# Three units share the first x tiles, and the unit of 36 features becomes 16 fp32 products on column halves

## The chip, the core and the metric

One Trainium2 chip, one of its cores. The metric is the device time of one launch in microseconds (us). The kernel's engines: TensorE does the matrix products (PE in the profile, its weight loads PEld), VectorE is DVE, ScalarE is ACT, GpSimd is POOL, and SyncE (SP) issues nearly all transfers from device memory.

## The reference

The kernel computes one layer of a hybrid encoder trunk on x of 256 tokens by 2048 features, in float32. Cut to what the change touches:

```python
u = _rms_norm(x, norm_mix_pre)                     # x * rsqrt(mean(x^2) + eps) * gain
proj = u @ w_in
sb, fox, rw, gates = _split(proj, ...)
q_a, k_a, v_a = _split(sb, (512,) * 3)             # stick-breaking attention, 4 heads of 128
q_b, k_b, v_b, f_b = _split(fox, ...)              # f_b: 4 forget logits per token
log_f = log_sigmoid(f_b + b_forget)
# RWKV-7: the projected features are mixed with those of the token before
z = z + (z_prev - z) * mu
r, k, v, wd, ad, gd = _split(z, (1024, 1024, 1024, 64, 64, 160))
g = sigmoid(gd) @ g_up
```

After that come the three mixers, three gated branches, an output projection with a second norm, and an MLP of 8192 hidden features. All of that is the same in both kernels.

## The kernel before

**A unit.** Nearly every projection is made in units of 128 output features. The weights of a unit are two pieces of the stream `wst`, each of 128 x 1024 floats (512 KB), and each piece covers eight of the 16 tiles of 128 input features. Products are not made in fp32: each operand is split into a rounded part ("hi", type fp32r) and the rest ("lo"). ACT writes the hi part of a weight piece (L173), DVE subtracts to get the lo part (L175). An input tile is split in the same way into a tile of 512 columns: the hi part of 256 tokens, then the lo part. A unit then needs, on PE, 16 products of hi weights with 512 columns (L191, the last one L197) and 16 of lo weights with 256 columns (L195). `evac` adds the two halves of the result (L249 on ACT, L250 on DVE).

**Streams and buffers.** SP issues the pieces in order into three `raw` tiles; a new piece waits until the lo part of the one three back is made. `whi` and `wlo` have three tiles each, and one piece is split ahead (`wnext`). Each `wnext` call that loads a piece also runs one function from the list `side`: constants, then the normalised x tiles.

**The begin.** x comes in transposed, as 16 tiles in eight transfers of 256 KB. The first two units (the first two heads of the stick-breaking q) are made from x tiles as they land: `xsplit` (L340, that is L259 on ACT and L260 on DVE) multiplies with the norm's gain and splits; the norm's factor per token, `rstd`, is not known yet and is multiplied into the results later (`scaled`, L465). The orders of PE, ACT and DVE are written out by hand in this part (L317 to L407): for each pair of x tiles, `high` (L345) and `low` (L349) of unit 0 and of unit 1. The pieces of these units come as column halves (pieces 0 and 2) and whole (pieces 1 and 3; piece 3 lies in a tile of the pool tag `m`). After the begin only PE keeps its written order; a scheduler orders ACT and DVE.

**Behind the begin.** Units 2 to 7 follow on the same x tiles. Between them lie the eight squares of x (L431 on ACT, seven adds L433 on DVE, in the tile `A6` of tag `b6`), the sum over features on PE behind unit 4 (L438), `rstd` (L440 to L275), and a small product that turns `rstd` into columns behind unit 6 (L457). Then comes v (`tok`, eight pieces, L235 and L220), and behind v the unit `zz`: 32 features of the gate LoRA and the four forget logits, 36 of its 128 columns, the others zero. It reads the normalised tiles `upk` and is made like any other unit; `shift` (L640) then mixes it with the token before. The units of the next projections follow. Mixer work is woven between the units by a count of ticks, four in a unit.

Of the kernel before, what the change touches and what calls it, by code (L numbers as in the profile page):

```python
# [11 lines left out]
F32 = mybir.dt.float32  # L12
F32R = mybir.dt.float32r
AF = mybir.ActivationFunctionType
ALU = mybir.AluOpType
# [3 lines left out]
T = 256  # L19
D = 2048  # L20
KT = 16
AHEAD = 1
SHARE = 0.88
HALF = 1024
# [7 lines left out]
PC = {}  # L32
# [20 lines left out]
def hybrid_block(ctx, tc, xt, x, gains, params, consts, lora, gup, wst, out):  # L53
    nc = tc.nc
    V, A, G, PE = nc.vector, nc.scalar, nc.gpsimd, nc.tensor

    cpool = ctx.enter_context(tc.tile_pool(name="cpool", bufs=1))
    wpool = ctx.enter_context(tc.tile_pool(name="wpool", bufs=1))
# [17 lines left out]
    def pk():  # L76
        return pkpool.tile([128, 512], F32R, tag="pk", name=nm("pk"), bufs=24)
# [6 lines left out]
    par = cpool.tile([128, NPAR], F32, name="par")  # L84
# [52 lines left out]
    def tick(f=1.0):  # L137
# [7 lines left out]
        if hooks:  # L145
# [3 lines left out]
    wpos = [0]  # L149


    gc = wst.shape[0] - 256 - 32 - 48
    jump = {23: 28, 53: 24, 27: 54, gc + 7: gc + 12, gc + 19: gc + 24, gc + 31: gc + 8,
            gc + 11: gc + 20, gc + 23: gc + 32}
    wq = []
    side = []

    rawdma = [None]

    def wraw(n=None):  # L160
# [9 lines left out]
    def wsplit(raw, n=None, now=True):  # L170
        hl = home[0](n) if home[0] else None
        hi, lo = hl or (wpool.tile([128, HALF], F32R, tag=t, name=nm(t), bufs=3) for t in ("whi", "wlo"))
        A.activation(hi, raw, AF.Copy)  # L173
        wq.append((hi, lo))
        low = lambda: V.tensor_tensor(lo, raw, hi.bitcast(F32), ALU.subtract)  # L175
        return low() if now else low
# [101 lines left out]
    rp = p1.enter_context(tc.tile_pool(name="rp", bufs=1))  # L278
# [7 lines left out]
    z = tmp()  # L286
    G.memset(z, 0.0)
    X0 = rp.tile([128, KT, T], F32, tag="SC", name="x0", bufs=1)
    A6 = rp.tile([128, 6, T], F32, tag="b6", name="a6", bufs=1)
    nc.scalar.dma_start(out=par, in_=params)  # L290

    dum = cpool.tile([128, 1], F32, name="dum")
# [3 lines left out]
    def xload(a, b):  # L296
        nc.sync.dma_start(out=X0[:, a:b, :], in_=xt[:, a:b, :])


    raws = {n: wpool.tile([128, HALF], F32, tag="raw", name=nm("raw"), bufs=3) for n in (0, 2)}  # L300
    for c in (0, 512):
        for n in (0, 2):
            nc.sync.dma_start(out=raws[n][:, c:c + 512], in_=wst[n][:, c:c + 512])
            xload(c // 128 + n, c // 128 + n + 2)
    raws[1] = wraw(1)
    xload(8, 10)
    xload(10, 12)

    raws[3] = rp.tile([128, 2, 512], F32, tag="m", name="raw3", bufs=4).rearrange("p a b -> p (a b)")
    nc.sync.dma_start(out=raws[3], in_=wst[3])  # L310
    xload(12, 14)
    xload(14, 16)
    cst = cpool.tile([128, 4], F32, name="cst")
# [11 lines left out]
    ps = mps()  # L325
# [16 lines left out]

    def high(u, *ks):
        for k in ks:
            PE.matmul(qb[u], w[u, k // 8][0][:, k % 8 * 128:k % 8 * 128 + 128], xpk[k], start=k == 0, stop=False)  # L345

    def low(u, *ks):
        for k in ks:
            PE.matmul(qb[u][:, 0:T], w[u, k // 8][1][:, k % 8 * 128:k % 8 * 128 + 128], xpk[k][:, 0:T], start=False,  # L349
                      stop=k == 15)  # L350

    qb = [gps() for _ in range(2)]
    w = {(u, 0): [wpool.tile([128, HALF], F32R, tag=t, name=nm(t), bufs=3) for t in ("whi", "wlo")] for u in range(2)}

    def part(u, c, lo):
        c = slice(c, c + 512)
        hi, raw = w[u, 0][0][:, c], raws[2 * u][:, c]
        if lo:
            V.tensor_tensor(w[u, 0][1][:, c], raw, hi.bitcast(F32), ALU.subtract)
        else:  # L360
            A.activation(hi, raw, AF.Copy)

    def both(u, *ks):
        high(u, *ks)
        low(u, *ks)

    for c in (0, 512):
        k = c // 128
        part(0, c, False)
        xsplit(k)  # L370
        xsplit(k + 1)
        part(1, c, False)
        high(0, k, k + 1)
        high(1, k, k + 1)
        part(0, c, True)
        if c == 0:
            part(1, c, True)
        low(0, k, k + 1)
        xsplit(k + 2)
        xsplit(k + 3)  # L380
        if c:
            part(1, c, True)
        low(1, k, k + 1)
        both(0, k + 2, k + 3)
        both(1, k + 2, k + 3)

    def whole(n):
        later = wsplit(raws.pop(n), None, False)
        return wq.pop(), later

    w[0, 1], later = whole(1)
    xsplit(8)
    xsplit(9)
    later()
    both(0, 8, 9)
    xsplit(10)
    xsplit(11)
    both(0, 10, 11)
    w[1, 1], later = whole(3)
    later()  # L400
    both(1, 8, 9, 10, 11)
    for k in (12, 14):
        xsplit(k)
        xsplit(k + 1)
        both(0, k, k + 1)
        both(1, k, k + 1)
    order.__exit__(None, None, None)  # L407
    order = tc.manual_schedule(engines={mybir.EngineType.PE})
    order.__enter__()
# [14 lines left out]
    wpos[0] = 4  # L424
    rstd = rp.tile([128, T], F32, tag="cs", name="rstd1", bufs=1)

    def square(i):
        xf = X0[:, 2 * i:2 * i + 2, :]
        b = 2 + 2 * (i % 2) if i else 0
        with tc.issue_after(behind[0].ins):  # L430
            A.activation(A6[:, b:b + 2, :], xf, AF.Square)  # L431
        if i:
            V.tensor_tensor(A6[:, 0:2, :], A6[:, 0:2, :], A6[:, b:b + 2, :], ALU.add)  # L433

# [10 lines left out]
    upk = [pk() for _ in range(KT)]  # L445
# [21 lines left out]
    todo = [lambda i=i: square(i) for i in range(8)] + [norm] + [lambda k=k: normed(k) for k in range(3)] + [column] +\  # L467
           [lambda k=k: normed(k) for k in range(3, 9)]
    for h, n in enumerate((0, 0, 4, 4, 1, 3, 4, 3)):
        ps = qb[h] if h < 2 else unit(xpk)  # L470
        qk.append(g1())
        behind[1] = evac(ps, qk[h])
        if h > 4:
            scaled(h)
        for f in todo[:n]:
            f()
        del todo[:n]

    def later(i):
        normed(9 + i)  # L480
        if i < 5:
            scaled(i)

    side.extend(lambda i=i: later(i) for i in range(7))
    done["sbq"], done["sbk"] = qk[:4], qk[4:]


# [70 lines left out]
    def fox_mix():  # L558
# [78 lines left out]
            yield ("stage", 0.8)  # L637
        done["yb"] = out

    def shift(ps, i, dst, n=128):  # L640

        b, t = tmp(), tmp()
        zp = rp.tile([128, T + 1], F32, tag="zp", name=nm("zp"), bufs=2)
        G.memset(zp[:, 0:1], 0.0)
        A.activation(b[0:n], ps[0:n, T:2 * T], AF.Copy)
        V.tensor_tensor(t[0:n], ps[0:n, 0:T], b[0:n], ALU.add)
# [331 lines left out]
    for br in ("sb", "fox"):  # L978
        for s in ("q", "k"):
            if br == "sb":  # L980
                continue
            lst = []
            for h in range(4):
                ps = unit(upk)
                t = g1()
                evac(ps, t)
                lst.append(t)
            done[br + s] = lst
        done[br + "v"] = vtok(br == "sb")
        done[br] = True  # L990
        for i, nme, n in ((0, "zx", 128), (1, "zy", 128)) if br == "fox" else ((2, "zz", 36),):
            ps = unit(upk)
            z = rp.tile([128, T], F32, tag="tha", name=nme, bufs=1) if i == 0 else \
                rp.tile([64 if n == 36 else n, T], F32, name=nme)
            shift(ps, MU_X + i, z[0:n], n)
            done[nme] = z
# [36 lines left out]
    for g in range(4):  # L1033
        m = rp.tile([128, 2, 512], F32, tag="m", name=nm("m"), bufs=4)
# [170 lines left out]
    low = more(False)  # L1205
# [454 lines left out]
```

## Time and profile before

| what | value |
|---|---|
| median of 3 runs | 1508.16 us (1507.34 to 1508.66) |
| the profiled execution, its own time | 1509.36 us |
| its span, first to last instruction | 1507.6 us |
| lies outside the span | 1.8 us |
| DVE busy | 1206.6 us (80%) |
| ACT busy | 939.8 us (62%) |
| DMA, mean over the span | 207 GB/s |

A busy engine is one with an instruction in work. A row of the timeline gives the start and the duration of a group of like instructions that follow each other, and how many there are; the last one's duration reaches into the next group's start, because products are pipelined. An fp32 product appears as two records of the PE, an fp32r product as one. The distance from one start to the next is therefore the cost of a product, not its duration.

### The profile page before, as it was taken

What the parts mean: (1) busy time and instruction counts of PE and PEld (TensorE: products, weight loads), DVE (VectorE), ACT (ScalarE), POOL (GpSimd) and SP (SyncE); (2) the same over time, 40 slices, a digit from 0 to 9 for tenths busy, and PEclk for the clock granted to TensorE, in tenths of its full rate; (3) what the DMA queues carried; (4) which work ended last, traced back from release to release, by engine and by line L of the source; (5) the groups of instructions that cost most, each with busy time, mean ns of one, the idle gap of its engine ahead of it and who ended that gap; (6) DMA issues with size and microseconds to landing.
All of it is one profiled execution on the core that took longest, in us unless ns stands there. A gap on an engine that the chain in (4) does not pass through costs nothing.

```text
span 1507.6 us, 22703 instructions
## 1 busy us (share of the span) xinstructions
PE 1492.0 (99%) x8384; PEld 1254.0 (83%) x8384; DVE 1206.6 (80%) x1673; ACT 939.8 (62%) x1433; POOL 94.5 (6%) x151
## 2 busy tenths in 40 slices
PE   9999999999999999999999999999999999999997
PEld 7888888887788887788888988888888888888886
DVE  7875679895678796476557778998899989999996
ACT  7665677545676445564545766776667666767663
POOL 0021003000001000000000000000000000000000
PEclk9999999999999999999999999999999999999999
DMA  7655454454455465456675768888888888989874
GB/s 263 197 168 184 142 182 154 154 182 163 156 165 177 154 192 186 130 169 196 231 238 159 265 177 254 229 242 273 263 259 258 244 254 248 258 254 258 246 224 152
DMA packets 104687, 312.71 MB, mean 207 GB/s; under 512 B 10240, under 2 KB 12288, under 8 KB 104576
## 3 DMA queue, kind: packets, MB, share of 16 engines
q1 hardware_dynamic: 93968, 279.87, 56.2%
q0 software_dynamic: 8064, 29.36, 10.5%
q10 hardware_dynamic: 2544, 2.03, 0.5%
q8 instruction: 66, 1.08, 0.3%
q14 instruction: 45, 0.37, 0.1%
HBM read 279.77 MB, written 2.10 MB: 187 GB/s over the span
## 4 chain that ended last, share of the span: by engine, by line
PE 89%; DMA 4%; DVE 2%; issue 2%; ACT 2%; POOLq 0%; SPq 0%; DVEq 0%; POOL 0%; ACTq 0%
PE gps L235 27%; PE gps L191 21%; PE gps L195 12%; PE gps L220 7%; PE mps L1378 3%; PE mps L1380 3%; PE mps L1379 3%; DMA raw<-in_wst_dram 2%; PE gps L1380 2%; PE gps L1378 2%; PE gps L1379 2%; DMA raw<-raw 2%; PE gps L197 1%; DVE wlo L175 1%; ACT whi L173 1%
## 5 line engine op out<-in xcount | busy, mean ns | idle before, releaser
L175 DVE TENSOR_TENSOR wlo<-raw,whi 128x1024 fp32r<-128x1024 f32 x576 | 699.0, 1224 | 159.2 <-ACT whi L173 147.3
L173 ACT ACTIVATE whi<-raw 128x1024 fp32r<-128x1024 f32 x576 | 604.1, 1057 | 260.4 <-PE gps L235 76.3
L191 PE MATMUL gps<-pk,whi 128*128 128x512 f32 x1479 | 375.6, 392 | 1.8 <-DVE tmp L1296 1.0
L191 PEld LDWEIGHTS gps<-pk,whi 128*128 128x128 f32 x1479 | 274.2, 188 | 57.9 <-ACT whi L173 2.3
L235 PE MATMUL gps<-whi,pk 128*128 128x512 f32 x1004 | 253.6, 393 | 0.0
L195 PEld LDWEIGHTS gps<-pk,wlo 128*128 128x128 f32 x1582 | 215.6, 190 | 15.6 <-DVE wlo L175 0.7
L195 PE MATMUL gps<-pk,wlo 128*128 128x256 f32 x1582 | 221.1, 283 | 0.1
L235 PEld LDWEIGHTS gps<-whi,pk 128*128 128x128 f32 x1004 | 186.6, 188 | 39.8 <-issue 1.0
L235 PE MATMUL gps<-wlo,pk 128*128 128x512 f32 x502 | 138.2, 393 | 0.1
L235 PEld LDWEIGHTS gps<-wlo,pk 128*128 128x128 f32 x502 | 93.2, 188 | 20.0 <-DVE wlo L175 0.5
L1378 PE MATMUL mps<-whi,fm 128*128 128x512 f32 x224 | 88.8, 396 | 0.8 <-ACT whi L173 0.6
L1295 ACT ACTIVATE tmp<-gps 128x256 f32<-128x256 f32 x64 | 24.6, 384 | 101.4 <-PE gps L197 99.5
L1379 PE MATMUL mps<-whi,fm 128*128 128x512 f32 x224 | 87.8, 392 | 0.0
L1380 PE MATMUL mps<-wlo,fm 128*128 128x512 f32 x224 | 87.6, 391 | 0.0
L1358 POOL DMA_DIRECT2D raw<-raw x56 | 48.8, 872 | 573.1 <-DVE raw L1355 279.5
L1355 DVE TENSOR_TENSOR raw<-raw,raw 128x1024 f32<-128x1024 f32 x56 | 68.5, 1222 | 0.8
L1378 PE MATMUL gps<-whi,fm 128*128 128x512 f32 x168 | 65.9, 392 | 0.0
L1380 PE MATMUL gps<-wlo,fm 128*128 128x512 f32 x168 | 65.9, 392 | 0.0
L1379 PE MATMUL gps<-whi,fm 128*128 128x512 f32 x168 | 65.5, 390 | 0.0
L220 PE MATMUL gps<-whi,pk 128*128 128x512 f32 x224 | 60.8, 393 | 0.0
L1380 PEld LDWEIGHTS mps<-wlo,fm 128*128 128x128 f32 x224 | 42.1, 188 | 9.7 <-DVE wlo L175 0.2
L1378 PEld LDWEIGHTS mps<-whi,fm 128*128 128x128 f32 x224 | 42.4, 189 | 8.9 <-ACT whi L173 2.9
(346 smaller groups left out, 1726.6 us busy)
## 6 DMA issues: line engine op xcount, KB each, us to landing
raw<-in_wst_dram SPq DMA_DIRECT2D x516, 512.0 KB, 4.4
raw<-raw POOLq DMA_DIRECT2D x56, 512.0 KB, 6.8
x<-in_xt_dram SPq DMA_DIRECT2D x8, 256.0 KB, 6.7
x<-in_x_dram SPq DMA_DIRECT2D x8, 256.0 KB, 4.7
raw<-in_wst_dram SPq DMA_DIRECT2D x4, 256.0 KB, 4.9
g<-in_gains_dram SPq DMA_DIRECT2D x4, 256.0 KB, 4.8
pk<-in_gains_dram SPq DMA_DIRECT2D x4, 256.0 KB, 6.9
out_dram<-x SPq DMA_DIRECT2D x4, 256.0 KB, 2.8
```

The source lines that it names most:

```text
L173: A.activation(hi, raw, AF.Copy)
L175: low = lambda: V.tensor_tensor(lo, raw, hi.bitcast(F32), ALU.subtract)
L191: PE.matmul(ps, hi[:, i * 128:i * 128 + 128], pks[i], start=first and i == 0, stop=False)
L195: PE.matmul(ps[:, 0:T], lo[:, i * 128:i * 128 + 128], pks[i][:, 0:T], start=False, stop=False)
L220: PE.matmul(ps[tt], pks[k][:, c:c + 128], w[:, (k - k0) * 512:(k - k0) * 512 + 512], start=k == 0 and part == 0 and w is hl[0], stop=w is ...
L235: PE.matmul(ps[tt], pks[k][:, c:c + 128], w[:, (k - k0) * 512:(k - k0) * 512 + 512], start=k == 0 and part == 0 and w is hl[0], stop=False)
L1295: A.activation(b, ps[:, T:2 * T], AF.Copy)
L1355: V.tensor_tensor(R[d, a], R[d, a], R[d, b], ALU.add)
L1358: G.dma_start(out=R[d, a], in_=R[d, b], accum_op=ALU.add)
L1378: PE.matmul(Q[f], a, w, start=d == d0 and i == 0, stop=False)
L1379: PE.matmul(Q[f], b, w, start=False, stop=False)
L1380: PE.matmul(Q[f], a, wl, start=False, stop=d == dn and i == 1)
```

## The change

Three things are changed.

1. The begin makes three units (0, 1, 2) from the arriving x tiles. All six of their pieces come as column halves of 256 KB, 20 transfers in all with x. The second pieces go to tiles of the pool `pk` (as raw data) and are split into six tiles of their own: four of tag `m`, one of `b6`, one of `Ti`. The tile `A6` for the squares, which is of tag `b6` too, is therefore taken later, behind the begin.
2. The unit `zz` is no longer a unit. Its stream pieces 28 and 29 are skipped. `few` loads the first 64 of each 128 columns into the tile `wz` (two transfers, 128 partitions x 8 rows of 64 floats each) and multiplies them with the gain. `narrow` then makes 16 fp32 products of 64 weight columns with the 256 tokens of the plain x tile `X0`; even tiles accumulate in result rows 0 to 63, odd ones in rows 64 to 127.
3. `shift` adds the two halves and multiplies with `rstd` where it has fewer than 64 rows.

```diff
-    jump = {23: 28, 53: 24, 27: 54, gc + 7: gc + 12, gc + 19: gc + 24, gc + 31: gc + 8,
+    jump = {23: 30, 53: 24, 27: 54, gc + 7: gc + 12, gc + 19: gc + 24, gc + 31: gc + 8,
...
-    A6 = rp.tile([128, 6, T], F32, tag="b6", name="a6", bufs=1)
...
-    raws = {n: wpool.tile([128, HALF], F32, tag="raw", name=nm("raw"), bufs=3) for n in (0, 2)}
-    for c in (0, 512):
-        for n in (0, 2):
-            nc.sync.dma_start(out=raws[n][:, c:c + 512], in_=wst[n][:, c:c + 512])
-            xload(c // 128 + n, c // 128 + n + 2)
-    raws[1] = wraw(1)
+    raws = {u: wpool.tile([128, HALF], F32, tag="raw", name=nm("raw"), bufs=3) for u in range(3)}
+
+    def wload(u, c):
+        nc.sync.dma_start(out=raws[u][:, c:c + 512], in_=wst[2 * u][:, c:c + 512])
+
+    wload(0, 0)
+    xload(0, 2)
+    wload(1, 0)
+    wload(2, 0)
+    xload(2, 4)
+    wload(0, 512)
+    xload(4, 6)
+    wload(1, 512)
+    xload(6, 8)
+    wload(2, 512)
+    seconds = {u: [pk().bitcast(F32) for _ in range(2)] for u in range(3)}
+
+    def sload(u):
+        for c in range(2):
+            rawdma[0] = nc.sync.dma_start(out=seconds[u][c], in_=wst[2 * u + 1][:, 512 * c:512 * c + 512])
+
+    sload(0)
     xload(8, 10)
     xload(10, 12)
-    raws[3] = rp.tile([128, 2, 512], F32, tag="m", name="raw3", bufs=4).rearrange("p a b -> p (a b)")
-    nc.sync.dma_start(out=raws[3], in_=wst[3])
+    sload(1)
+    sload(2)
     xload(12, 14)
     xload(14, 16)
...
+    more2 = [rp.tile([128, HALF], F32R, tag=t, name=nm("w2"), bufs=n) for t, n in
+             (("m", 4), ("m", 4), ("m", 4), ("m", 4), ("b6", 1), ("Ti", 1))]
...
-    for c in (0, 512):
-        k = c // 128
-        part(0, c, False)
-        xsplit(k)
-        xsplit(k + 1)
-        part(1, c, False)
-        high(0, k, k + 1)
-        high(1, k, k + 1)
-        part(0, c, True)
...
+    part(0, 0, False)
+    two(0)
+    part(0, 0, True)
+    part(1, 0, False)
+    high(0, 0, 1)
+    part(1, 0, True)
+    high(1, 0, 1)
+    part(2, 0, False)
+    low(0, 0, 1)
+    low(1, 0, 1)
+    part(2, 0, True)
+    both(2, 0, 1)
+    two(2)
+    for u in range(3):
+        both(u, 2, 3)
+    part(0, 512, False)
+    part(0, 512, True)
+    two(4)
+    part(1, 512, False)
+    part(1, 512, True)
+    both(0, 4, 5)
+    two(6)
+    both(0, 6, 7)
+    part(2, 512, False)
+    part(2, 512, True)
+    both(1, 4, 5, 6, 7)
+    whole(0)
+    two(8)
+    both(2, 4, 5, 6, 7)
+    both(0, 8, 9)
+    two(10)
+    both(0, 10, 11)
+    whole(1)
+    both(1, 8, 9, 10, 11)
+    whole(2)
+    two(12)
+    both(2, 8, 9, 10, 11)
+    two(14)
     for k in (12, 14):
-        xsplit(k)
-        xsplit(k + 1)
-        both(0, k, k + 1)
-        both(1, k, k + 1)
+        for u in range(3):
+            both(u, k, k + 1)
...
-        ps = qb[h] if h < 2 else unit(xpk)
+        ps = qb[h] if h < 3 else unit(xpk)
...
+    def few():
+        wz.append(rp.tile([128, KT, 64], F32, tag="m", name="wz", bufs=4))
+        for h in range(2):
+            nc.sync.dma_start(out=wz[0][:, 8 * h:8 * h + 8, :],
+                              in_=wst[28 + h].rearrange("p (a b) -> p a b", a=8)[:, :, 0:64])
+        V.tensor_tensor(wz[0], wz[0], par[:, PC["g1"]:PC["g1"] + KT].unsqueeze(2).to_broadcast([128, KT, 64]), ALU.mult)
+
     side.extend(lambda i=i: later(i) for i in range(7))
+    side.append(few)
...
+    def narrow():
+        ps = gps()
+        for k in range(KT):
+            c = 64 * (k % 2)
+            PE.matmul(ps[c:c + 64, 0:T], wz[0][:, k, :], X0[:, k, :], start=k < 2, stop=k >= KT - 2)
+        return ps
...
+        if n < 64:
+            A.activation(b[0:n], ps[64:64 + n, 0:T], AF.Copy)
+            V.tensor_tensor(b[0:n], ps[0:n, 0:T], b[0:n], ALU.add)
+            V.tensor_tensor(t[0:n], b[0:n], rstd[0:n], ALU.mult)
...
-            ps = unit(upk)
+            ps = unit(upk) if n == 128 else narrow()
```

The `two`, `whole` and `part` of the new text are small: `two(k)` splits x tiles k and k+1, `part` splits a column half of a first piece, `whole(u)` splits the second piece of unit u in two halves, hi on ACT and lo on DVE.

**PE at the begin**, from its first product on x. `gps_125` and `gps_126` are the results of units 0 and 1 before, `gps_135`, `gps_136` and `gps_137` those of units 0, 1 and 2 now; the tiles named `xpk` are the split x tiles in the order of their arrival. Before:

```order
L345 MATMUL gps_125<-xpk_132,whi_127 128x512
L345 MATMUL gps_125<-xpk_135,whi_127 128x512
L345 MATMUL gps_126<-xpk_132,whi_129 128x512
L345 MATMUL gps_126<-xpk_135,whi_129 128x512
L349 MATMUL gps_125<-xpk_132,wlo_128 128x256
L349 MATMUL gps_125<-xpk_135,wlo_128 128x256
L349 MATMUL gps_126<-xpk_132,wlo_130 128x256
L349 MATMUL gps_126<-xpk_135,wlo_130 128x256
L345 MATMUL gps_125<-xpk_147,whi_127 128x512
```

The same place in the changed program:

```order
L359 MATMUL gps_135<-xpk_151,whi_138 128x512
L359 MATMUL gps_135<-xpk_154,whi_138 128x512
L359 MATMUL gps_136<-xpk_151,whi_140 128x512
L359 MATMUL gps_136<-xpk_154,whi_140 128x512
L363 MATMUL gps_135<-xpk_151,wlo_139 128x256
L363 MATMUL gps_135<-xpk_154,wlo_139 128x256
L363 MATMUL gps_136<-xpk_151,wlo_141 128x256
L363 MATMUL gps_136<-xpk_154,wlo_141 128x256
L359 MATMUL gps_137<-xpk_151,whi_142 128x512
L359 MATMUL gps_137<-xpk_154,whi_142 128x512
L363 MATMUL gps_137<-xpk_151,wlo_143 128x256
L363 MATMUL gps_137<-xpk_154,wlo_143 128x256
```

Where unit 0 went on with the third x tile (`xpk_147`), unit 2 now comes in between on the first two.

**PE behind v.** The result `gps_664` is the second half of v before; the unit `zz` follows it there (`gps_846`), with mixer products (L498, L499) woven in:

```order
L220 MATMUL gps_664<-wlo_805,pk_248 128x512
L191 MATMUL gps_846<-pk_264,whi_826 128x512
L191 MATMUL gps_846<-pk_265,whi_826 128x512
L191 MATMUL gps_846<-pk_266,whi_826 128x512
L191 MATMUL gps_846<-pk_267,whi_826 128x512
L191 MATMUL gps_846<-pk_268,whi_826 128x512
L191 MATMUL gps_846<-pk_269,whi_826 128x512
L498 MATMUL mps_861<-g_48_281,g_80_457 128x256
```

Now the 16 products of `narrow` stand there, and the next unit, the first of the second attention's q (`gps_892`), takes the mixer products:

```order
L220 MATMUL gps_679<-wlo_820,pk_291 128x512
L684 MATMUL gps_865<-x_82,wz 64x256 x16
L191 MATMUL gps_892<-pk_324,whi_841 128x512
L191 MATMUL gps_892<-pk_325,whi_841 128x512
L191 MATMUL gps_892<-pk_326,whi_841 128x512
L191 MATMUL gps_892<-pk_327,whi_841 128x512
L191 MATMUL gps_892<-pk_328,whi_841 128x512
L191 MATMUL gps_892<-pk_329,whi_841 128x512
L537 MATMUL mps_907<-g_59_341,g_84_472 128x256
```

Some 275 rows further on the mixer products are back at their old distance from the units, and from there to the end PE's order is what it was.

**DVE around the norm.** The multiplication of `wz` stands between the result of unit 4 and the first step of `rstd` (L469, which is L440 before):

```order
L175 TENSOR_TENSOR wlo_492<-raw_489,whi_491 128x1024
L250 TENSOR_TENSOR g_84_472<-gps_427,tmp_473 128x256
L520 TENSOR_TENSOR wz<-wz,par 128x1024
L469 TENSOR_SCALAR tmp_479<-mps_476 128x256
L175 TENSOR_TENSOR wlo_514<-raw_511,whi_513 128x1024
L175 TENSOR_TENSOR wlo_554<-raw_551,whi_553 128x1024
```

So `rstd` and the lo parts of unit 6 (`wlo_514`, `wlo_554`) are queued behind it on DVE, in order.

More of the change, by code (lines that the diff above doesn't have):

```diff
@@ L350, in low @@
                       stop=k == 15)
-    qb = [gps() for _ in range(2)]
-    w = {(u, 0): [wpool.tile([128, HALF], F32R, tag=t, name=nm(t), bufs=3) for t in ("whi", "wlo")] for u in range(2)}
+    qb = [gps() for _ in range(3)]
+    w = {(u, 0): [wpool.tile([128, HALF], F32R, tag=t, name=nm(t), bufs=3) for t in ("whi", "wlo")] for u in range(3)}
+    more2 = [rp.tile([128, HALF], F32R, tag=t, name=nm("w2"), bufs=n) for t, n in
+             (("m", 4), ("m", 4), ("m", 4), ("m", 4), ("b6", 1), ("Ti", 1))]
     def part(u, c, lo):
         c = slice(c, c + 512)
-        hi, raw = w[u, 0][0][:, c], raws[2 * u][:, c]
+        hi, raw = w[u, 0][0][:, c], raws[u][:, c]
         if lo:
@@ L365, in both, with two, whole @@
         low(u, *ks)
-    for c in (0, 512):
-        k = c // 128
-        part(0, c, False)
+    def two(k):
         xsplit(k)
         xsplit(k + 1)
-        part(1, c, False)
-        high(0, k, k + 1)
-        high(1, k, k + 1)
-        part(0, c, True)
[L376 to L394, printed above, removed]
+    def whole(u):
+        hi, lo = w[u, 1] = more2[2 * u:2 * u + 2]
+        for c in range(2):
+            cs = slice(512 * c, 512 * c + 512)
+            A.activation(hi[:, cs], seconds[u][c], AF.Copy)
+            V.tensor_tensor(lo[:, cs], seconds[u][c], hi[:, cs].bitcast(F32), ALU.subtract)
+    part(0, 0, False)
[27 more added lines that the diff above has]
+    both(2, 4, 5, 6, 7)
     both(0, 8, 9)
-    xsplit(10)
-    xsplit(11)
+    two(10)
     both(0, 10, 11)
-    w[1, 1], later = whole(3)
-    later()
+    whole(1)
     both(1, 8, 9, 10, 11)
+    whole(2)
+    two(12)
+    both(2, 8, 9, 10, 11)
+    two(14)
     for k in (12, 14):
-        xsplit(k)
-        xsplit(k + 1)
-        both(0, k, k + 1)
-        both(1, k, k + 1)
+        for u in range(3):
+            both(u, k, k + 1)
     order.__exit__(None, None, None)
@@ L423, in hybrid_block @@
     side.append(lambda: const(con, consts[:, 128 + NR:]))
-    wpos[0] = 4
+    wpos[0] = 6
+    A6 = rp.tile([128, 6, T], F32, tag="b6", name="a6", bufs=1)
     rstd = rp.tile([128, T], F32, tag="cs", name="rstd1", bufs=1)
@@ L482, in later @@
             scaled(i)
+    wz = []
+    def few():
[4 more added lines that the diff above has]
+        V.tensor_tensor(wz[0], wz[0], par[:, PC["g1"]:PC["g1"] + KT].unsqueeze(2).to_broadcast([128, KT, 64]), ALU.mult)
     side.extend(lambda i=i: later(i) for i in range(7))
+    side.append(few)
     done["sbq"], done["sbk"] = qk[:4], qk[4:]
@@ L644, in shift @@
         G.memset(zp[:, 0:1], 0.0)
-        A.activation(b[0:n], ps[0:n, T:2 * T], AF.Copy)
-        V.tensor_tensor(t[0:n], ps[0:n, 0:T], b[0:n], ALU.add)
+        if n < 64:
+            A.activation(b[0:n], ps[64:64 + n, 0:T], AF.Copy)
+            V.tensor_tensor(b[0:n], ps[0:n, 0:T], b[0:n], ALU.add)
+            V.tensor_tensor(t[0:n], b[0:n], rstd[0:n], ALU.mult)
+        else:
+            A.activation(b, ps[:, T:2 * T], AF.Copy)
+            V.tensor_tensor(t, ps[:, 0:T], b, ALU.add)
         A.activation(zp[0:n, 1:T + 1], t[0:n], AF.Copy, scale=P("mu", i, slice(0, n)))
```

## The prediction

> **What bounds the kernel now.** I read the page's shares first, then the busy time by stretches, then the timeline of the first 30 us. Of a stretch I quote start and end, length, and the busy time of each engine:
>
> ```profile
> PE 1492.0 (99%) x8384; PEld 1254.0 (83%) x8384; DVE 1206.6 (80%) x1673; ACT 939.8 (62%) x1433; POOL 94.5 (6%) x151
> ...
> 6.00:11.00 5.00, 3.93 (x19) 2.81 (x17) 2.96 (x7) 2.92 (x7) 0.00 (x0) 1.00 0.92 335
> 11.00:16.00 5.00, 3.94 (x19) 2.83 (x19) 4.39 (x9) 4.69 (x10) 0.00 (x0) 1.00 1.02 402
> 16.00:21.40 5.40, 5.40 (x31) 4.51 (x31) 5.40 (x10) 4.98 (x11) 0.00 (x0) 1.00 0.80 306
> 26.95:60.00 33.05, 33.05 (x186) 28.97 (x185) 26.92 (x48) 22.14 (x35) 0.00 (x0) 1.00 0.60 188
> ...
> 1200.00:1507.60 307.60, 296.99 (x1463) 248.98 (x1461) 276.57 (x325) 194.93 (x267) 24.07 (x28) 0.99 0.82 239
> ```
>
> PE is the bound from 16 us on, at a granted clock of 1.00. Only the begin has real holes; the 10.6 us without PE after 1200 us lie almost all in the closing stores. So a microsecond of PE work or of PE waiting taken out early should come off the end, unless something behind it then runs late. Between 6 and 16 us PE is waiting while the transfers are full (share 0.92 and 1.02): there the arrival of x sets the pace, through ACT and DVE.
>
> The timeline gives the cost of a unit and of the begin (start, duration, count):
>
> ```profile
> 5.93 1.27 PE L345 MATMUL gps<-xpk,whi 128*128 128x512 f32 x4
> ...
> 26.95 2.00 PE L191 MATMUL gps<-xpk,whi 128*128 128x512 f32 x8
> ...
> 86.17 2.00 PE L191 MATMUL gps<-pk,whi 128*128 128x512 f32 x8
> 88.01 1.12 PE L195 MATMUL gps<-pk,wlo 128*128 128x256 f32 x8
> 88.96 1.78 PE L191 MATMUL gps<-pk,whi 128*128 128x512 f32 x7
> ...
> 91.76 1.54 PE L191 MATMUL gps<-pk,whi 128*128 128x512 f32 x6
> ```
>
> From one unit's first product to the next one's: 91.76 - 86.17 = 5.59 us. A hi product costs (88.01 - 86.17)/8 = 0.23, a lo product (88.96 - 88.01)/8 = 0.119; for a pair of x tiles a unit pays 2 x (0.23 + 0.119) = 0.698 us. Units 0, 1 and 2 are done before: 26.95 is the first product of unit 3. From 5.93 that is 21.0 us for 3 x 8 x 0.698 = 16.75 us of products, so 4.3 us of holes are there to be won.
>
> **The change: the begin.** I go through its written order by hand. ACT and DVE steps, start to start:
>
> ```profile
> 7.76 0.91 ACT L259 ACTIVATE xpk<-x,par 128x256 fp32r<-128x256 f32 x2 [1.63 <-DMA x<-in_xt_dram]
> 8.60 0.63 ACT L361 ACTIVATE whi<-raw 128x512 fp32r<-128x512 f32 x1
> ...
> 10.23 0.88 DVE L260 SCALAR_TENSOR_TENSOR xpk<-x,par,xpk 128x256 fp32r<-128x256 f32 x2 [1.05 <-ACT xpk L259]
> 11.03 0.68 DVE L359 TENSOR_TENSOR wlo<-raw,whi 128x512 fp32r<-128x512 f32 x1
> 11.63 0.87 DVE L260 SCALAR_TENSOR_TENSOR xpk<-x,par,xpk 128x256 fp32r<-128x256 f32 x2
> ```
>
> A pair of x tiles costs ACT 0.84 and DVE 0.80, a column half of weights 0.55 (estimated from its 0.63) and 0.60. Arrivals: issue times of the queue, and the transfer view's time from issue to landing of the fourth, fifth and seventh piece of 256 KB and of a late one (8.60):
>
> ```profile
> 2.12 0.43 SPq L297 DMA_DIRECT2D x<-in_xt_dram  x1
> 2.59 0.43 SPq L303 DMA_DIRECT2D raw<-in_wst_dram  x1
> ...
> 3.54 0.43 SPq L303 DMA_DIRECT2D raw<-in_wst_dram  x1
> ...
> 8.60 1.41 SPq L297 DMA_DIRECT2D x<-in_xt_dram  x2
> ...
> x<-in_xt_dram SPq DMA_DIRECT2D x1, 256.0 KB, 5.6
> raw<-in_wst_dram SPq DMA_DIRECT2D x1, 256.0 KB, 6.0
> raw<-in_wst_dram SPq DMA_DIRECT2D x1, 256.0 KB, 6.8
> x<-in_xt_dram SPq DMA_DIRECT2D x1, 256.0 KB, 6.8
> ```
>
> Landings: fourth 7.72, fifth 8.59, seventh 10.34, and the one issued at 8.60, which is the 15th in steps of 256 KB, at 15.4: (15.4 - 10.34)/8 = 0.63 us a step. I take it that the queue delivers the new list at the same pace. Then x tiles 2 and 3, now fifth, land at 8.6 (before 7.7); tiles 4 and 5, seventh, at 10.3; tiles 6 and 7, ninth, at 11.6; the twentieth and last at 18.5.
>
> Now the passage. Unit 2's first weights, fourth, land at 7.7; ACT and DVE split them by 8.4 and 9.1, so PE, done with units 0 and 1 on the first pair at 7.6, makes unit 2's from 8.45. Tiles 2 and 3 are split by 10.0; three units on them last to 11.9. Unit 0 on tiles 4 and 5 to 12.6. Tiles 6 and 7 are split at 12.9 and 13.3, since ACT has unit 1's weights ahead of them: PE waits, and ends unit 0 on this pair at 13.8. From there I find PE never short: 16 pairs of 0.698 are left (6 + 6 for units 1 and 2, 4 for unit 0), 11.2 us, to 25.0. What they need is ready ahead: DVE delivers tiles 8 and 9 at 15.9 (wanted 16.6), 10 and 11 at 16.7 (17.3), unit 1's second lo part at 17.9 (18.9), unit 2's at 19.1 (20.3), tiles 12 and 13 at 19.9 (20.9), 14 and 15 at 20.7 (23). The holes that remain are those before 13.8: a third unit gives PE something to do in the later ones. **Gain 26.95 - 25.0 = 1.95 us.** Bounds: 4.3 (no hole at all); nothing, if x comes 2 us later than I take it to, since half the transfers ahead of the third pair are now weights.
>
> **The change: narrow.** It removes one unit, 5.59 us of PE, with two 512 KB transfers and two splits (1.22 DVE and 1.06 ACT each by the page's rows below, all under PE). It adds 16 fp32 products with 64 weight columns and 256 moving ones. Full-width fp32 products and products on alternating column halves stand in the trace, both with 128 moving columns:
>
> ```profile
> 79.77 0.38 PE L499 MATMUL mps<-g,g 128*128 128x128 f32 x2
> 79.99 0.60 PE L498 MATMUL mps<-g,g 128*128 128x256 f32 x2
> 80.42 0.39 PE L499 MATMUL mps<-g,g 128*128 128x128 f32 x2
> ...
> L805 PEld LDWEIGHTS mps<-con,g x64: 132/137/138, 285.1 to 520.7; 128*64 128x64 f32 x64
> ...
> 285.11 1.97 PE L805 MATMUL mps<-con,g 128*64 128x128 f32 x32
> 287.01 0.73 PE L191 MATMUL gps<-pk,whi 128*128 128x512 f32 x2
> ```
>
> At full width a record of 128 columns costs (79.99 - 79.77)/2 = 0.11, of 256 columns (80.42 - 79.99)/2 = 0.215. On the halves, 32 records take 1.90 to the next line's start, 0.059 each: two neighbours share the array. With 256 columns that makes 32 x 0.215/2 = 3.44 us, and the excess of L805 over half price, 32 x (0.059 - 0.055) = 0.13, for getting in and out: 3.6 us. Bounds: 3.44, and 32 x 0.215 = 6.9 if nothing is shared. I take 3.6, as L805 is the same form with half the columns. **Gain 5.6 - 3.6 = 2.0 us**, between 2.15 and a loss of 1.3.
>
> In L805 a weight load lasts 137 ns (the middle number of its row), yet the records follow each other at 59: the loads lie under the products of the other half. The Trainium skill (TensorE: Matmul & The Clock Gate, Part 3: Packing small matmuls) states that a weight load overlaps products in flight only where its row group differs, and here all tiles use all rows. By that rule a record would cost its 0.1075 and its load, 32 x (0.1075 + 0.137) = 7.8 us, and `narrow` would lose 2.2; this trace disagrees.
>
> **What costs nothing, and under what.** I count from 25.0, the first product of unit 3.
>
> ```profile
> L175 DVE TENSOR_TENSOR wlo<-raw,whi 128x1024 fp32r<-128x1024 f32 x576 | 699.0, 1224 | 159.2 <-ACT whi L173 147.3
> L173 ACT ACTIVATE whi<-raw 128x1024 fp32r<-128x1024 f32 x576 | 604.1, 1057 | 260.4 <-PE gps L235 76.3
> ...
> 17.43 1.14 ACT L431 ACTIVATE a<-x 128x512 f32<-128x512 f32 x2
> ...
> 20.90 0.69 DVE L433 TENSOR_TENSOR a<-a 128x512 f32<-128x512 f32 x1
> ```
>
> *The squares* wait for the tile `b6` until then; before, they began at 17.4. The sum over features on PE comes behind unit 4, at 25.0 + 11.2 = 36.2. Eight squares (1.14/2 = 0.57 each) and seven adds (0.6 of their 0.69, as for the lo halves of that shape) have to fit under two units beside four splits: I find the last add done at 35.3, so 0.9 us of cover; whatever is later than that, PE waits. *`rstd`* and what follows:
>
> ```profile
> 39.26 0.42 DVE L440 TENSOR_SCALAR tmp<-mps 128x256 f32<-128x256 f32 x1
> ...
> 45.44 0.42 DVE L275 TENSOR_TENSOR rstd<-rstd,tmp 128x256 f32<-128x256 f32 x1
> ...
> 50.17 0.50 PE L457 MATMUL mps<-ident,rstd 128*128 128x4 f32 x4
> ...
> q10 hardware_dynamic: 528, 0.43, 12.4%
> ```
>
> The chain takes 45.86 - 39.26 = 6.6 us, and its column product came at 50.17; now it comes behind unit 6, at 48.0, so the chain must start by 41.4, and the multiplication of `wz` (128x1024, priced like a lo split, 1.2) by 40.2. `wz`'s second transfer is issued behind the piece of unit 5, when the lo part of unit 4's first piece frees its `raw` tile, at about 30. Its price: no transfer of rows of 256 bytes is in the trace. Last row above, from the stretch 58 to 70: 528 small packets (0.8 KB) took 12.4% of 16 engines, 45 ns each. `wz` has 2048 rows: 2048 x 45/16 = 5.8 us of the transfer engines, less than the 33 x 0.40 = 13 us they have free between 27 and 60. With the longest landing quoted, 6.8, it is there near 37; behind it on DVE stand `rstd` and unit 6's lo parts, and PE behind both. Cover 3 us. *DVE* has the same work in 5.6 us less of PE time, less two splits; I walked its order to the end of v and find each lo part of v's pieces 2 to 3 us early. *`shift`* adds one 0.4 us multiplication of 36 rows. *The mixers* begin one unit later and have caught up before fox's v.
>
> The Trainium skill (DMA: Bandwidth & Descriptors, the table at its head) gives 512 bytes as the least transfer for full rate, without a price; the 45 ns are of packets above that, and no run here shows 256-byte rows.
>
> **Sum.** 1.95 + 2.0 = 3.95 off 1509.36, the profiled execution's own time (span 1507.6 and 1.8 around it): 1505.4. The median of the runs stands 1.2 below it: 1508.16 - 3.95 = **1504.2 us**. I count 0.2%, 3.0 us, as the least difference from no change that a measurement of this kernel tells.
>
> **Rivals.** *Arrival decides (0.2).* If x tiles 6 and 7 land a microsecond or more later than 11.6, every microsecond moves the 13.8, and the begin gives 0 to 0.9. For it: ACT's wait of 1.63 in its row above, and the fuller queue of weights. Against: the same bytes a microsecond as before. With `narrow` whole: 1505.3 to 1506.2, within 0.2%.
>
> *The halves do not share (0.05).* Then `narrow` costs 6.9, 1.3 more than the unit, and what is left is 1.95 - 1.3 = 0.65: 1507.5; with weight loads in the open on top (7.8), 1508.4. L805 speaks against it, though with 128 moving columns, not 256.
>
> *`wz` comes late, slower (0.13).* Its two transfers stand in SP's queue ahead of the pieces of units 5 and 6, with eight rows a partition where all others have one or two; its landing holds DVE, DVE holds `rstd`, and PE stops at the column product. The stall is the landing less 40.2. At 44.2 both gains are gone, and from 47.2 the kernel is slower by over 0.2%. If each issue takes eight times the 0.43 of other transfers (two times 3.4 from 27.3, when SP comes to the first, and a piece between), the landing 6.8, the packets 5.8 and two full pieces ahead of them 4 x 0.63, then it lands at 27.3 + 6.9 + 0.4 + 6.8 + 5.8 + 2.5 = 49.7: 1508.16 - 3.95 + 9.5 = 1513.7. Against: all of these would have to come together.
>
> **Chances.** Forecast with both gains, a stall of under a microsecond included: 0.62. Arrival 0.2, halves 0.05, `wz` late 0.13, of which 0.03 stays within 0.2%. Faster 0.62, within 0.2% 0.2 + 0.05 + 0.03 = 0.28, slower 0.10. Range: low 1502.2, from 2 us more of the begin's 4.3; high 1507.6, which takes in arrival and halves. The forecast's own range is 1502.2 to 1505.2.
>
> **What would show it.** Right: the first product of unit 3 at 25.0 +- 0.6; PE's last holes at 8, 9 and 13 us; `narrow` 3.6 us from its start to the next line's, 32 records of 64 columns; no PE wait between 25 and 90. Wrong: unit 3 at 26 or later with ACT waiting for x; `narrow` near 7; PE waiting before the sum over features or the column product, and a DVE idle ahead of `wz` that a transfer ended. If these all come out as said and the end is not 3 to 4 us earlier, the argument that PE's time carries through is what failed.

## The result, and the profile after

The changed kernel takes 1504.55 us (median of 12 runs, 1503.16 to 1505.64), the kernel before beside it 1508.13 (12 runs, 1507.12 to 1511.04). The ratio is 0.9975, with a 95% interval of 0.9968 to 0.9983: 3.6 us less, between 2.6 and 4.8. Predicted were 1504.2 us and a range of 1502.2 to 1507.6. The profiled execution took 1505.64 us, its span is 1503.8 (before: 1509.36 and 1507.6).

The page's shares, of the changed kernel:

```profile
PE 1489.7 (99%) x8384; PEld 1250.7 (83%) x8384; DVE 1206.8 (80%) x1677; ACT 938.4 (62%) x1435; POOL 91.1 (6%) x151
```

By stretches, of the changed kernel (start and end, length, busy time of PE, its weight loads, DVE, ACT, POOL, granted clock, share and GB/s of the transfers):

```profile
6.00:11.00 5.00, 4.96 (x23) 3.71 (x24) 3.98 (x8) 3.29 (x7) 0.00 (x0) 1.00 0.95 307
11.00:16.00 5.00, 4.62 (x23) 3.40 (x22) 4.96 (x11) 4.99 (x12) 0.00 (x0) 1.00 1.05 399
...
25.00:60.00 35.00, 35.00 (x196) 30.55 (x195) 32.27 (x58) 27.10 (x45) 0.00 (x0) 1.00 0.58 188
60.00:100.00 40.00, 40.00 (x220) 33.19 (x219) 30.18 (x45) 22.89 (x33) 4.21 (x6) 1.00 0.49 162
```

Between 6 and 16 us PE was busy for 7.87 us of the 10; now it is for 9.58, and makes 46 products there, not 38. The transfers deliver no more than before (307 and 399 GB/s now, 335 and 402 then): the third unit takes pieces that the stream brought next before, and works on x tiles that came anyway. From 25 to 100 us PE has no gap.

The timeline of PE after (start, duration, count, and in brackets the idle time and what ended it):

```profile
6.04 1.36 PE L359 MATMUL gps<-xpk,whi 128*128 128x512 f32 x4
...
11.32 0.90 PE L359 MATMUL gps<-xpk,whi 128*128 128x512 f32 x2
...
12.84 0.90 PE L359 MATMUL gps<-xpk,whi 128*128 128x512 f32 x2 [0.38 <-DVE xpk L260]
...
13.82 1.09 PE L359 MATMUL gps<-xpk,whi 128*128 128x512 f32 x4
...
25.01 2.00 PE L191 MATMUL gps<-xpk,whi 128*128 128x512 f32 x8
...
76.13 3.67 PE L684 MATMUL gps<-x,wz 128*64 128x256 f32 x32
79.73 1.65 PE L191 MATMUL gps<-pk,whi 128*128 128x512 f32 x6
81.22 0.59 PE L537 MATMUL mps<-g,g 128*128 128x256 f32 x2
...
88.06 2.00 PE L191 MATMUL gps<-pk,whi 128*128 128x512 f32 x8
```

Unit 3 begins at 25.01 (before 26.95), and the holes end at 13.82: from there 11.19 us, which is 16 pairs of 0.698. `narrow` lasts from 76.13 to 79.73, 3.60 us. The unit that began at 91.76 before, the second of the second attention's q (the q unit, from here on), begins at 88.06, 3.70 earlier; the spans differ by 3.8. So in these two executions the whole gain is there at 88 us, and nothing behind it gives it back. All that PE waits for in this execution (total, times, longest) is short:

```profile
PE mps L1430 <- ACT whi L173: 1.3, 2, 0.7
PE mps L341 <- POOL dum L292: 1.1, 1, 1.1
PE gps L191 <- ACT whi L173: 0.8, 2, 0.5
PE gps L359 <- DVE xpk L260: 0.4, 1, 0.4
PE gps L191 <- DVE tmp L1348: 0.2, 1, 0.2
```

The fourth row is the hole at 12.84; no row belongs to the sum over features or to the column product.

### The profile page after: what moved, and what is told of

Its sections match the earlier page's. It is cut to its first block, busy times and chain, and to the rows that moved or that the text cites. A ratio compares the mean times of both kernels' runs of the same rounds, so it can differ in the third digit from the quotient of the medians.

```text
span 1503.8 us, 22719 instructions
## 1 busy us (share of the span) xinstructions
PE 1489.7 (99%) x8384; PEld 1250.7 (83%) x8384; DVE 1206.8 (80%) x1677; ACT 938.4 (62%) x1435; POOL 91.1 (6%) x151
## 4 chain that ended last, share of the span: by engine, by line
PE 94%; DVE 2%; ACT 1%; issue 1%; DMA 0%; SPq 0%; POOLq 0%; DVEq 0%; POOL 0%; ACTq 0%
PE gps L235 27%; PE gps L191 22%; PE gps L195 12%; PE gps L220 7%; PE mps L1430 3%; PE mps L1432 3%; PE mps L1431 3%; PE gps L1432 2%; PE gps L1430 2%; PE gps L1431 2%; PE gps L197 2%; DVE wlo L175 1%; PE mps L836 1%; PE gps L359 1%; PE gps L1219 1%
## 5 line engine op out<-in xcount | busy, mean ns | idle before, releaser
L175 DVE TENSOR_TENSOR wlo<-raw,whi 128x1024 fp32r<-128x1024 f32 x570 | 691.3, 1223 | 151.5 <-ACT whi L173 141.8
L173 ACT ACTIVATE whi<-raw 128x1024 fp32r<-128x1024 f32 x570 | 597.9, 1057 | 246.5 <-PE gps L235 71.7
L191 PE MATMUL gps<-pk,whi 128*128 128x512 f32 x1460 | 370.7, 392 | 1.0 <-ACT whi L173 0.8
L191 PEld LDWEIGHTS gps<-pk,whi 128*128 128x128 f32 x1460 | 270.6, 188 | 56.4 <-ACT whi L173 1.7
L195 PE MATMUL gps<-pk,wlo 128*128 128x256 f32 x1561 | 218.0, 282 | 0.1
```

Of the source, the lines that this page charges most:

```text
L191: PE.matmul(ps, hi[:, i * 128:i * 128 + 128], pks[i], start=first and i == 0, stop=False)
L195: PE.matmul(ps[:, 0:T], lo[:, i * 128:i * 128 + 128], pks[i][:, 0:T], start=False, stop=False)
```

## The experiments

**The parts alone.** The first kernel has the new begin and the old unit `zz`, the second the old begin and `narrow`.

```diff
 begin only (against the change)
-    jump = {23: 30, ...
+    jump = {23: 28, ...
...
-    side.append(few)
...
-        if n < 64:
+        if n < 0:
...
-            ps = unit(upk) if n == 128 else narrow()
+            ps = unit(upk)

 narrow only (against the kernel before)
-    jump = {23: 28, ...
+    jump = {23: 30, ...
...
+    side.append(few)
...
-            ps = unit(upk)
+            ps = unit(upk) if n == 128 else narrow()
```

In the second, `few`, `narrow` and the new lines of `shift` are those of the change.

> The change without narrow: the 36 features are made as a full unit again, the begin keeps its three units. Theory (each part's PE time comes off the end by itself): the first product of unit 3 at 25.0 us, the unit of 36 features 5.6 us again, 1508.1 - 1.9 = 1506.2 us. Rival (the parts help each other, the shorter unit covering what the begin loses later): 1507.5 or more, with PE waits between 25 and 90 us.

> The kernel before with narrow alone: two units in the begin, 16 fp32 products on column halves for the 36 features. Theory: narrow 3.7 us in place of 5.6, the rest shifted, 1508.1 - 1.9 = 1506.2 us, and the multiplication of wz not waiting for its transfer. Rival (the squares come earlier here, so the gain of narrow was bought by the begin's order, or DVE runs late): no gain, 1508.

The begin alone: 1506.84 us (11 runs, ratio 0.9989, 0.9980 to 0.9998). `narrow` alone: 1506.97 us (11 runs, ratio 0.9992, 0.9983 to 1.0001). The kernel before took 1508.22 beside them (33 runs). The timelines of PE, of the begin alone first:

```profile
24.35 2.00 PE L191 MATMUL gps<-xpk,whi 128*128 128x512 f32 x8
...
35.94 1.13 PE L467 MATMUL mps<-a,cr 128*128 128x256 f32 x4 [0.25 <-DVE a L462]
...
89.67 2.00 PE L191 MATMUL gps<-pk,whi 128*128 128x512 f32 x8
```

and of `narrow` alone:

```profile
78.16 3.67 PE L655 MATMUL gps<-x,wz 128*64 128x256 f32 x32
81.76 1.65 PE L191 MATMUL gps<-pk,whi 128*128 128x512 f32 x6
...
90.09 2.00 PE L191 MATMUL gps<-pk,whi 128*128 128x512 f32 x8
```

At the q unit the begin alone is 2.09 ahead and `narrow` alone 1.67; together 3.76, against 3.70 with both. The parts add up, though so closely only by luck: the begin alone had unit 3 at 24.35, 0.66 earlier than the change, and lost 0.5 of that behind it. The medians say 1.4 and 1.25; their intervals (0.3 to 3.0, and -0.2 to 2.6) hold the terms of the prediction too, and by its time alone `narrow` is not clear of no change. In the first timeline the sum over features, L467, would follow two units behind 24.35, at 24.35 + 2 x 5.59 = 35.53; it begins at 35.94, 0.41 late, 0.25 of it put down to the last add of the squares. The cover that the prediction put at 0.9 is used up there, for a reason of this kernel's own: on DVE a lo part (L175, at 34.06) stands between the last two adds, which in the change follow each other.

**Do the column halves share the array?** All 16 products go to one half, with the same operands. They accumulate in one result, and the add of the halves is dropped; nothing is halved or doubled, other than the expectation says:

```diff
-            c = 64 * (k % 2)
-            PE.matmul(ps[c:c + 64, 0:T], wz[0][:, k, :], X0[:, k, :], start=k < 2, stop=k >= KT - 2)
+            PE.matmul(ps[0:64, 0:T], wz[0][:, k, :], X0[:, k, :], start=k == 0, stop=k == KT - 1)
...
-            A.activation(b[0:n], ps[64:64 + n, 0:T], AF.Copy)
-            V.tensor_tensor(b[0:n], ps[0:n, 0:T], b[0:n], ALU.add)
+            A.activation(b[0:n], ps[0:n, 0:T], AF.Copy)
```

> The changed kernel with all 16 products of narrow on result rows 0 to 63, so that no two of them lie on different column halves. The 36 features come out as half the sum of both halves would: the second operand of shift's sum is the same 36 rows, so they are doubled before rstd. Theory (sharing of the array by the halves is what makes narrow cheap): 32 records of 0.215 us, narrow 6.9 to 7.0 us, 1504.5 + 3.3 = 1507.8 us. Rival A (64 columns are cheap by themselves): narrow stays near 3.7, 1504.5. Rival B (weight loads lie in the open on one half): 32 x (0.215 + 0.137) = 11.3 us, 1512.1 us.

Measured 1507.94 us (11 runs, ratio 1.0001, 0.9992 to 1.0010). The timeline of PE, of this kernel:

```profile
75.64 7.12 PE L683 MATMUL gps<-x,wz 128*64 128x256 f32 x32
82.69 1.65 PE L191 MATMUL gps<-pk,whi 128*128 128x512 f32 x6
```

The durations of its weight loads (least, middle, longest in ns; first and last start in us), of this kernel:

```profile
L683 PEld LDWEIGHTS gps<-x,wz x32: 132/137/137, 75.6 to 82.2; 128*64 128x64 f32 x32
```

and the loads of the changed kernel:

```profile
L684 PEld LDWEIGHTS gps<-x,wz x32: 132/137/137, 76.1 to 79.2; 128*64 128x64 f32 x32
```

The loads last the same in both; only their first and last starts tell the kernels apart. On one half the line takes 7.05 us, 0.220 a record: the full price of 256 columns. Alternating, it takes 3.60 us, 0.1125 a record. So half the width gives no discount by itself; the alternation does, and without it `narrow` is dearer than the unit of 5.59. Rival B falls as well: 32 loads in the open would have made 11.3, so the loads are hidden on one half too. The end moves by the whole difference: 7.05 - 3.60 = 3.45 in the trace, 3.4 between the medians, 1507.94 and 1504.55 (the kernel before beside them 1508.22 and 1508.13). Against the kernel before, the change takes 2.6 to 4.8 less and this one between 1.2 less and 1.5 more: the two intervals do not meet, but they are wide. This is also the most direct test that a microsecond of PE work at 76 us comes off the end.

**What fills the hole at 13 us?** In the changed kernel's trace ACT splits unit 1's weights (11.05) ahead of x tiles 6 and 7 (11.57). The next kernel loads and splits these tiles first; the one after it also puts x tiles 0 and 1 ahead of the first weights.

```diff
 x ahead
-    wload(1, 512)
     xload(6, 8)
+    wload(1, 512)
...
-    part(1, 512, False)
-    part(1, 512, True)
     both(0, 4, 5)
     two(6)
+    part(1, 512, False)
+    part(1, 512, True)

 x first (as x ahead, and)
-    wload(0, 0)
     xload(0, 2)
+    wload(0, 0)
...
-    part(0, 0, False)
     two(0)
+    part(0, 0, False)
```

> The changed kernel with the fourth x transfer (tiles 6 and 7) issued ahead of the second half of unit 1's first weights, and split ahead of them on ACT and DVE; PE's order is the same. Theory (the hole before 13.8 us is the arrival and splitting of tiles 6 and 7 behind weights that PE needs later): that hole goes, unit 0 ends on this pair at 13.0, the first product of unit 3 comes at 24.2 to 24.4 instead of 25.0, 1503.8 us. Rival (the transfer engines' start-up sets all landings, the order in the queue does not matter): 25.0 and 1504.5 us.

> As the run with tiles 6 and 7 ahead, and the first x transfer (tiles 0 and 1) issued as the very first, split before the first weights. Theory (each hole of the begin has its own arrival in front of it; the one before 6 us is tiles 0 and 1): the first product comes at 5.4 to 5.6 instead of 6.1, the first product of unit 3 at 23.3 to 23.6, and 0.3 to 0.5 us less than that run in the time. Rival (a later step sets the end, such as tiles 2 and 3 at 8.9): unit 3 at 23.9 as there, no difference in the time.

x ahead: 1504.07 us (10 runs, ratio 0.9975, 0.9965 to 0.9984). Its trace has no hole behind 10 us, as the theory of the order had it, and unit 3 at 23.86, earlier than its 24.2 to 24.4. x first: 1504.26 us (6 runs, ratio 0.9971, 0.9959 to 0.9982); its first product came later than the change's 6.04, not earlier, and its unit 3 at 23.85. The two timelines of PE, x ahead and then x first, and then ACT's first step on x in x first:

```profile
23.86 2.00 PE L191 MATMUL gps<-xpk,whi 128*128 128x512 f32 x8
```

```profile
6.57 1.38 PE L359 MATMUL gps<-xpk,whi 128*128 128x512 f32 x4
```

```profile
5.08 0.91 ACT L259 ACTIVATE xpk<-x,par 128x256 fp32r<-128x256 f32 x2 [2.41 <-DMA par<-in_params_dram]
```

In x first ACT waited 2.41 us for the parameters (`par`, which hold the gain), and split the first weights only behind that. PE, too, was until 6.57 on products whose result nothing reads (L341, from 1.10 on). So this run does not test what an earlier arrival of tiles 0 and 1 is worth; its theory stays open.

No gain of either shows in the time, though unit 3 came 1.15 earlier. So the changed kernel, as it is, and x ahead were run once more, beside x first:

> The changed kernel itself, beside the two reordered ones on the same chip: 1504.5 us, unit 3 between 24.3 and 25.1, since three executions with this begin gave 25.01, 24.35 and 24.52.

> The kernel with tiles 6 and 7 ahead once more, beside the changed kernel: unit 3 at 23.9, 0.6 to 1.1 us below the changed kernel of this batch, if PE's time carries through to the end; the same time as it if the end is set elsewhere.

The change again: 1504.24 us (7 runs, ratio 0.9971, 0.9960 to 0.9982). x ahead again: 1505.18 us (10 runs, ratio 0.9978, 0.9969 to 0.9987). The kernel before took 1507.91 beside them (17 runs). The timelines of PE, of the change again and then of x ahead again:

```profile
11.76 0.76 PE L359 MATMUL gps<-xpk,whi 128*128 128x512 f32 x2
...
12.60 1.09 PE L359 MATMUL gps<-xpk,whi 128*128 128x512 f32 x4
...
23.79 2.00 PE L191 MATMUL gps<-xpk,whi 128*128 128x512 f32 x8
```

```profile
24.44 2.00 PE L191 MATMUL gps<-xpk,whi 128*128 128x512 f32 x8
```

Neither came out as expected: the change reached unit 3 ahead of the 24.3 to 25.1 said for it, and x ahead came at 24.44 for 23.9, with a median 0.9 above the change's, not 0.6 to 1.1 below it (the intervals overlap). The order alone does not make the hole. The same code as the change, in another execution, has lost most of it and reaches unit 3 at 23.79, earlier than either execution of x ahead (23.86, 24.44). What differs is seen on ACT. First the changed kernel's execution beside the result, then the change again; the four x tiles that matter are 4 and 5, then 6 and 7:

```profile
7.73 0.91 ACT L259 ACTIVATE xpk<-x,par 128x256 fp32r<-128x256 f32 x2 [0.75 <-DMA x<-in_xt_dram]
...
10.24 0.91 ACT L259 ACTIVATE xpk<-x,par 128x256 fp32r<-128x256 f32 x2 [0.91 <-DMA x<-in_xt_dram]
11.05 0.61 ACT L377 ACTIVATE whi<-raw 128x512 fp32r<-128x512 f32 x1
11.57 0.89 ACT L259 ACTIVATE xpk<-x,par 128x256 fp32r<-128x256 f32 x2
```

```profile
8.97 0.91 ACT L259 ACTIVATE xpk<-x,par 128x256 fp32r<-128x256 f32 x2
...
10.31 0.89 ACT L259 ACTIVATE xpk<-x,par 128x256 fp32r<-128x256 f32 x2
```

In the first, ACT waits 0.91 us for tiles 4 and 5 and starts them at 10.24; in the second it does not wait and starts them at 8.97. Behind that ACT runs without a pause, so tiles 6 and 7 are 1.26 apart and unit 3 1.22. The begin alone and the one-half kernel have the same begin, and their timelines give two more pairs:

| execution | ACT starts tiles 4 and 5 | unit 3 | difference |
|---|---|---|---|
| the change | 10.24 | 25.01 | 14.77 |
| begin alone | 9.58 | 24.35 | 14.77 |
| one half | 9.78 | 24.52 | 14.74 |
| the change again | 8.97 | 23.79 | 14.82 |

Four executions, one constant, 14.74 to 14.82: when tiles 4 and 5 are at ACT sets when the begin ends. With x ahead it is another step. There PE has no gap behind its first products on tiles 2 and 3 (at 8.91 and 9.50), so tiles 4 to 7 set nothing. ACT's start on tiles 2 and 3, in x ahead:

```profile
7.83 0.91 ACT L259 ACTIVATE xpk<-x,par 128x256 fp32r<-128x256 f32 x2 [0.72 <-DMA x<-in_xt_dram]
```

From there to unit 3 it is 23.86 - 7.83 = 16.03 us, and in x ahead again 24.44 - 8.42 = 16.02. In the four executions of the change's begin the same distance is between 16.17 (the change again) and 17.28 (beside the result). So the order takes away the wait for tiles 4 to 7, where there is one: 0.15 us against the change again, 1.26 against the other. What that is worth in an average run, no time here tells from nothing; none of the variants is shown to beat the change.

## Why the prediction was right

**What bounds it.** PE's time carries through to the end, as far as the intervals tell: 3.70 gained at 88 us is 3.6 in the medians (2.6 to 4.8), and the 3.45 given back on one half is 3.4 in the medians. That the spans agree too, with 3.8, is luck. From the q unit's first product to the end, the nine profiled executions take between 1414.0 us (`narrow` alone, 1504.1 - 90.09) and 1416.3 (the change again, 1503.1 - 86.84); the two compared lie within 0.1 of each other.

**The begin.** Predicted 1.95, measured 1.94 in the execution beside the result, with unit 3 at 25.01 for 25.0 and unit 0 done on tiles 6 and 7 at 13.82 for 13.8. The walk of the order, with prices and landings of the old trace, had the last hole right: tiles 4 and 5, said to land at 10.3, came to ACT at 10.24, unit 1's weights behind them, and then tiles 6 and 7. Two things in it were less firm than the number. Tiles 2 and 3 came at 7.73, not 8.6, so the three units were done on them and unit 0 was on tiles 4 and 5 at 11.32, not 11.9; PE then stood the longer for tiles 5 to 7, and nothing was won. And the agreement to 0.01 is in part luck: over the four executions of this begin the gain, against the one profiled begin of before, is 1.94, 2.60, 2.43 and 3.16. The prediction's +- 0.6 was too narrow on the early side. The one other execution of the old begin, in `narrow` alone, does not show such a change: its unit 2 starts at 21.45, in the kernel before at 21.36.

**`narrow`.** Predicted 3.6, measured 3.60 from its start to the next line's, in both kernels that have it. The net is less than the 2.0 of the sum, for the price of getting in and out lies outside that distance. In: v's last two products begin at 75.58 and take 0.45, as the two from 74.22 to 74.67 in the first rows below; they are over at 76.03, and `narrow` starts at 76.13, 0.10 later. Out: the six hi products behind `narrow` take 81.22 - 79.73 = 1.49, the six in the same place before took 79.34 - 77.97 = 1.37 (second rows, of the kernel before), 0.12 less. So the change saves 5.59 - 3.60 - 0.22 = 1.77. The gain at the q unit less the gain at unit 3 says the same: 3.70 - 1.94 = 1.76, and in the change again, whose q unit begins at 86.84, 4.92 - 3.16 = 1.76. The prediction had put both prices into L805's excess over half price, 0.13, inside that line's own 1.90; behind L805, too, two hi products take 0.57 to the next line (287.01 to 287.58), not 0.46. That is the term that was mis-sized, and the sum with it: 3.70 for 3.95.

```profile
74.22 0.62 PE L220 MATMUL gps<-wlo,pk 128*128 128x512 f32 x2
74.67 1.07 PE L220 MATMUL gps<-whi,pk 128*128 128x512 f32 x4
75.58 0.61 PE L220 MATMUL gps<-wlo,pk 128*128 128x512 f32 x2
```

```profile
77.97 1.52 PE L191 MATMUL gps<-pk,whi 128*128 128x512 f32 x6
79.34 0.59 PE L498 MATMUL mps<-g,g 128*128 128x256 f32 x2
```

The rival that the halves do not share would have cost 6.9; the experiment that takes the sharing away measured 7.05, so its price was right and its premise wrong. The rule of the Trainium skill (TensorE: Matmul & The Clock Gate, Part 3) that a weight load overlaps products in flight only where its row group differs does not hold here: loads of 137 ns lie in steps of 112.5 ns, with all rows in use. On one half they lie in steps of 220 ns at no added cost, so the prediction's reading, that the loads lie under the products of the other half, is too narrow: products of the same half hide them as well.

**What costs nothing.** The squares, `wz` and `rstd`, of the changed kernel; first DVE, then PE:

```profile
34.12 1.48 DVE L462 TENSOR_TENSOR a<-a 128x512 f32<-128x512 f32 x2
...
36.80 0.42 DVE L250 TENSOR_TENSOR g<-gps,tmp 128x256 f32<-128x256 f32 x1
37.14 1.22 DVE L520 TENSOR_TENSOR wz<-wz,par 128x1024 f32<-128x1024 f32 x1
...
45.67 0.42 DVE L275 TENSOR_TENSOR rstd<-rstd,tmp 128x256 f32<-128x256 f32 x1
```

```profile
36.19 1.02 PE L467 MATMUL mps<-a,cr 128*128 128x256 f32 x4
...
48.23 0.50 PE L486 MATMUL mps<-ident,rstd 128*128 128x4 f32 x4
```

The last add ends at 35.6, the sum over features starts at 36.19: 0.6 of cover, where 0.9 was predicted. It is the thinnest cover of the change; in the begin alone, with its other order on DVE, it was gone, at a cost of 0.4. The multiplication of `wz` runs at 37.14 straight behind L250, waiting for no transfer; `rstd` is done at 46.1 for a column product at 48.23 (predicted 48.0).

**`wz` late.** This rival was priced too high. The issues on SP, of the changed kernel:

```profile
26.81 0.65 SPq L518 DMA_DIRECT2D wz<-in_wst_dram  x1
30.01 0.67 SPq L518 DMA_DIRECT2D wz<-in_wst_dram  x1
```

Its transfer view from 24 to 40 us (count, size, median us from issue to landing):

```profile
raw<-in_wst_dram SPq DMA_DIRECT2D x6, 512.0 KB, 3.9
wz<-in_wst_dram SPq DMA_DIRECT2D x2, 256.0 KB, 4.1
```

One transfer of `wz` costs SP 0.66 us, not eight times 0.43, and is there after 4.1 us: the second at about 34.2, where the prediction took 37 and the rival 49.7. The 2048 short rows did no harm that PE shows; still, 256 KB of them took as long to land as 512 KB of the pieces beside them.

**Arrival decides.** Its mechanism is real, by the table of the four executions: a microsecond of tiles 4 and 5 is a microsecond of the end of the begin. The prediction set it on the landing of tiles 6 and 7; there ACT waited for no transfer in any of the four. In the three later executions it moved the begin to the early side, so the gain was not lost. What remains open is how the begin of an average run compares with that of the profiled one: the interval of the result, 2.6 to 4.8, holds both a begin gain of 1.9 and one of 2.5.

## What to carry to other kernels

While data arrives and the matrix engine waits between the pieces, one more consumer of the same pieces can fill the holes: walk the written order with the prices of the old trace, and look for the one arrival behind which the chain has no slack. Small fp32 products of 64 weight columns are worth alternating between the column halves, since two neighbours then cost about one; on one half they paid the full width here, and a short run of them also pays some 0.2 us for getting in and out. And before crediting a reordering that moves the begin by a microsecond, profile the unchanged code again: here it moved by as much on its own.

## What the runs showed of the hardware

The first transfers of a launch vary from one execution of the same code to the next. The transfer of x tiles 4 and 5, issued at 3.54 us each time, took 6.7 us in the execution of the result and 5.4 us in the second execution of the same kernel (transfer view from 3.5 to 3.6 us, one for each):

```profile
x<-in_xt_dram SPq DMA_DIRECT2D x1, 256.0 KB, 6.7
```

```profile
x<-in_xt_dram SPq DMA_DIRECT2D x1, 256.0 KB, 5.4
```

What makes it so was not tried. Beyond the begin, single executions differ too: the begin alone is 2.09 ahead of before at the q unit, but 3.8 at the end. Of the 1.7 in between, 1.0 is a single stop in the profiled execution of before, between 900 and 1200 us (L191, for DVE's L1296), where this one has no gap; the rest was not traced. That execution of before is also 1.2 above its kernel's median, and the changed kernel's beside the result 1.1 above its own, so a difference of two spans is no measure of a term of 2 us; the distances inside the trace are.
